# A hybrid delta-net, RWKV and expert layer: two ring sizes, and the place of the first branch's merge products

## The chip, the cores and the metric

The kernel runs on one core of one Trainium2 chip. The metric is the device time of one execution in microseconds (us), and the time of a kernel is the median of its runs. One further execution was profiled; all rows of the trace come from it.

## The reference, cut to what matters

One layer over 256 latent tokens and 256 context tokens of width 1024. A projection feeds two recurrent branches (a gated delta net and RWKV-7), each runs over the context first and then, from the state so reached, over the latent tokens, in both directions. Their outputs are gated and merged, and a mixture of experts follows.

```python
s = s * ge_c[..., None, None] + jnp.einsum('...ck,...cv->...kv', kd_c, v_new)      # delta net, one chunk of 64
v_new = u_c - jnp.einsum('...ck,...kv->...cv', w_c, s)
o_c = jnp.einsum('...ck,...kv->...cv', qd_c, s) + jnp.einsum('...ij,...jv->...iv', qk_c, v_new)
...
y = jax.nn.sigmoid(g_a) * (o_a @ w_o_a) + jax.nn.sigmoid(g_b) * (o_b @ w_o_b)
return y @ w_out
...
hid = jax.nn.silu(jnp.einsum('td,edf->tef', t, w_gate[grp])) * jnp.einsum('td,edf->tef', t, w_up[grp])
out = out + jnp.einsum('tef,efd->td', hid * combine[:, grp, :, None], w_down[grp])
```

There are 32 experts with 3 MB of weights each, and every one is read in full.

## The kernel before

The whole program is unrolled. The code says what is computed in which tiles; a scheduler then fixes each engine's order, by priorities (`hi("gs")` raises one) and by when a pool of tiles finds room in the on-chip memory. Each engine, and the queue SP that issues most of the transfers, works its list strictly in order.

The stages, in the order in which they pass on TensorE (PE):

- Projections of both branches, the RWKV recurrence over the context (`rwkv_step(0, ...)`, four steps) and over the latent tokens (`rwkv_step(1, ...)`, four steps), with the delta net's preparation between them. A latent step multiplies keys with queries (`akps`), masks them on VectorE (DVE) into four tiles of the ring `arb`, forms `rps` and `ups`, copies to `ruv`, and ends with the outputs `yps`. The delta net's key-query products are `kqp`; they read `gq` and `gk`.
- The delta net's eight chunk steps, `gdn_step(0..7)`. A step loads `gkc` and `gvc` (steps 4 to 7 also `gqc`), transposes them on PE (`gkt`, `gvt`), scales them to `gkd` on DVE and `gr` on ScalarE (ACT), subtracts the state's part (`gks`, then DVE on `gr`), solves (`gup`, copied by ACT to `guu`) and updates the state (`gsp`, added on DVE to `gS`, which GpSimd (POOL) has decayed first). Latent steps also make the output `gop`, copied to `gr`, transposed as `got`, added to `yo`. Their tiles live in the pool `gx`, which in the kernel before opens where the recurrence's pools have closed. `gkt`, `gvt` and `got` share a single PSUM buffer.
- Beside these steps, the remaining gate projections (`pj`) and conditioning products (`ada`), whose weights come through a ring of tiles named `w`: 10 tiles of 256 KB in the main pool (`NB['w']`), 12 in a second pool (`w2`) in this stage.
- `rwkv_post`: a norm over the RWKV output (`mean` twice, `ysq`, `yc`) and its gate.
- `merge_b`: the first of the two branches to be merged, eight groups of products `pab` from `yc`, each read by DVE into `tbs`.
- `gdn_post` (`gon`), a small product `shp`, then `merge_a` (`pab` from `post`), the output projection (`acc`), residual and router.
- The experts, four at a time: gather (`xsp`), gate and up (`gup` from `wgu`), down (`dnp` from `wd`). `wgu` has 6 slots of 2 MB and `wd` 7 of 1 MB. Parts of the first experts' weights are loaded ahead, during the merges, where room opens.

`merge_b` is written ahead of the steps, and `gdn_step` has raised priority, so that the scheduler mixes the two.

Of the kernel before, what the change touches and what calls it, by code (L numbers as in the profile page):

```python
# [17 lines left out]
P = 128  # L18
# [82 lines left out]
class K:  # L101
    def __init__(self, ctx, tc, A, dbg=None):
        self.nw = NB["w"]
        self.ctx, self.tc, self.nc, self.A, self.dbg = ctx, tc, tc.nc, A, dbg or {}
# [55 lines left out]
    def e(self, name, *dims, rows=P):  # L160
        return self.t(self.pe, name, *dims, tag="e", bufs=NB["e"], w=520, rows=rows)

    def rt(self, name, *dims):
        return self.t(self.prt, name, *dims, tag="rt", bufs=NB["rt"], w=520)

# [65 lines left out]
    def ada_first(self, hf, pool):  # L231
        ps = self.psum(NB["at"][0], name="ada0")[:, 0:512]

# [8 lines left out]
        self.nc.vector.tensor_copy(a, ps)  # L242
        pt = self.psum(NB["at"][1], name="adat")
        for j in range(4):
# [9 lines left out]
    def ada_rest(self, i, tags):  # L254
# [5 lines left out]
        if q == 0:  # L260
            self.copy(self.arow[b], ps, NB["aa"])
        else:
# [340 lines left out]
    def rwkv_step(self, seg, s, T):  # L603
# [6 lines left out]
        V = X[:, 1024:1536].rearrange("p (j a n) -> p j a n", j=4, a=2)  # L610
# [6 lines left out]
        if upd:  # L617
# [8 lines left out]
            if S is not None:  # L626
                Sp = self.t(self.pst, "rS", 2, 4, C, bufs=1)
                for e in range(2):
                    r = slice(64 * e, 64 * e + 64)
# [5 lines left out]
        nc.vector.tensor_copy(uv[0:64, 1, :], ps[0:64, :])  # L635


        arb = lambda: self.t(self.prx, "arb", 512, bufs=8)
        if seg:
            m = self.cst("mkr").rearrange("p (d x) -> p d x", d=2).unsqueeze(2).to_broadcast([P, 2, 2, 2 * C])  # L640
            rb = [[arb().rearrange("p (d j x) -> p d j x", d=2, j=2) for e in range(2)] for p in range(2)]
            for p in range(2):
                pvs = [self.psum("ch", name="akps").rearrange("p (d j x) -> p d j x", d=2, j=2) for e in range(2)]
                for d in range(2):
                    for j in range(2):
                        for e in range(2):
                            r = slice(64 * e, 64 * e + 64)
# [5 lines left out]
        else:  # L653
            pvs = [self.psum("ch", name="akps")[:, 0:4 * C].rearrange("p (j n) -> p j n", n=C) for e in range(2)]
            for j in range(4):
                for d in range(2):
                    ko = 64 * (1 - d)
                    for e in range(2):
                        r = slice(64 * e, 64 * e + 64)
# [8 lines left out]
        for h in range(8):  # L668
            e, j = h % 2, h // 2
# [20 lines left out]
        if upd:  # L690
# [4 lines left out]
            for h in range(8):  # L695
                r = slice(64 * (h % 2), 64 * (h % 2) + 64)
# [4 lines left out]
            for e in range(2):  # L701
                r = slice(64 * e, 64 * e + 64)
                self.copy(self.RSb[r, :, :, 64 * e:64 * e + 64], sv[r], e)

        if seg:
            yp = self.psum("ch", name="yps")
            yv = yp.rearrange("p (d j n) -> p d j n", d=2, j=4)
            for h in range(8):
                e, j = h % 2, h // 2
                r = slice(64 * e, 64 * e + 64)  # L710
# [269 lines left out]
    def gdn_step(self, s, T, tmp):  # L980
        nc = self.nc
        lat = s >= 4
        S = self.GS
        x = lambda name, *dims, bufs=2, pool=tmp: self.t(pool, name, *dims, bufs=bufs)
        KT, GV, QE = x("gkc", NH, 2, C, bufs=NB["gk"]), x("gvc", NH, 2, C, bufs=NB["gk"]), None
        nc.sync.dma_start(KT, self.kscr[s])
        nc.sync.dma_start(GV, self.vscr[s])
        if lat:
            QE = x("gqc", NH, 2, C, bufs=NB["gq"])
            nc.sync.dma_start(QE, self.escr[s - 4])  # L990
        v4 = lambda x: x.rearrange("p (h n) -> p h n", h=NH)
        ps = self.psum("pp", name="gkt")
        for h in range(NH):
            self.tr(ps[:, h * P:(h + 1) * P], KT[:, h].rearrange("p a n -> p (a n)"))
        kd = x("gkd", NH, P)
        self.tt(kd, v4(ps), self.kdc[:, s, :].unsqueeze(2).to_broadcast([P, NH, P]))
        ps = self.psum("pp", name="gvt")
        for h in range(NH):
            self.tr(ps[:, h * P:(h + 1) * P], GV[:, h].rearrange("p a n -> p (a n)"))
        r1 = x("gr1", NH, P, pool=self.gkeep)  # L1000
        for h in range(NH):
            self.act(r1[:, h, :], ps[:, h * P:(h + 1) * P], scale=self.bt[:, s, h:h + 1])
        if S is not None:
            ps = self.psum("gc", name="gks")
            for h in range(NH):
                for d in range(2):
                    self.mm(ps[64 * d:64 * d + 64, h * P:(h + 1) * P], KT[:, h, d, :], S[:, d, h, :])
            for h in range(NH):
                self.stt(r1[:, h, :], ps[:, h * P:(h + 1) * P], self.nbe[:, s, h:h + 1], r1[:, h, :],
                         ALU.mult, ALU.add)  # L1010
        ps = self.psum("gc", name="gup")
        for h in range(NH):
            for d in range(2):
                r = slice(64 * d, 64 * d + 64)
                self.mm(ps[r, h * P:(h + 1) * P], T[r, s * NH + h, :], r1[r, h, :])
        u = x("guu", NH, P)
        self.act(u, v4(ps))
        if s < 7:
            Sn = x("gS", 2, NH, P)
            if S is not None:  # L1020
                self.tt(Sn, S, self.sdec[:, :, :, s:s + 1].to_broadcast([P, 2, NH, P]), eng=nc.gpsimd)
            pss = [self.psum("gc", name="gsp") for _ in range(2)]

            for h in range(NH):
                for d in range(2):
                    r = slice(64 * d, 64 * d + 64)
                    self.mm(pss[d][:, h * P:(h + 1) * P], kd[r, h, :], u[r, h, :])
            for d in range(2):
                if S is None:
                    nc.vector.tensor_copy(Sn[:, d], v4(pss[d]))  # L1030
                else:
                    self.tt(Sn[:, d], Sn[:, d], v4(pss[d]), ALU.add)
            self.GS = Sn
        if lat:

            ps = self.psum("gc", name="gop")
            for h in range(NH):
                for d in range(2):
                    self.mm(ps[64 * d:64 * d + 64, h * P:(h + 1) * P], QE[:, h, d, :], S[:, d, h, :], start=h == 0,
                            stop=False)  # L1040
            for h in range(NH):
                for d in range(2):
                    r = slice(64 * d, 64 * d + 64)
                    self.mm(ps[r, h * P:(h + 1) * P], self.AQ[r, s - 4, h, :], u[r, h, :], start=False, stop=h == NH - 1)
            o = x("gr1", NH, P, pool=self.gkeep)
            self.act(o, v4(ps))
            ps = self.psum("pp", name="got")
            for h in range(NH):
                self.tr(ps[:, h * P:(h + 1) * P], o[:, h, :])
            pv = ps.rearrange("p (h d n) -> p h d n", h=NH, d=2)  # L1050
            for d in range(2):
                c0 = (s - 4) * C if d == 0 else L - (s - 3) * C
                dst = self.GO[:, :, c0:c0 + C]
                src = pv[:, :, d, :] if d == 0 else pv[:, :, d, ::-1]
                if s < 6:
                    self.act(dst, src)
                else:
                    self.tt(dst, dst, src, ALU.add)
# [388 lines left out]
EP0 = ((("wgu", 1), ("wd", 0)), (("wgu", 2), ("wd", 1)))  # L1447
EP1 = (("wgu", 3), ("wgu", 4), ("wd", 2))
PRE = (("wgu", 0), ("wgu", 1), ("wgu", 2), ("wd", 0), ("wgu", 3), ("wd", 1), ("wd", 2), ("wd", 3))
NB = {'st': 2, 'ys': 'PP', 'yc': [1, 1], 'hn': 'VAVA', 'im': 'AAPP', 'e': 7, 'rt': 13, 'w': 10, 'e1': 4, 'o2': 2, 'kvr': 2, 'cv': 'PVVPPVPPPVVV', 'g1': 3, 'g2': 0, 'imt': 1, 'gi': 0, 'hi': {'p00': 2500, 'p01': 2500, 'i0': 2500, 'gp': 2000, 'R': 2000, 'i': 2000, 'gs': 2000, 'I': 2000, 'J': 2000, 'p11': 200, 'j0': 1500, 'g': 400, 'V': -400, 'rw': 2000}, 'zf': 1, 'g0': 1, 'pe': 0, 'vr': 'vr', 'jt': 'pp', 'go': 'KGGgGGRRGRRikIVGQqJrrrrG', 'rX': 1, 'rbk': 2, 'ixt': 1, 'vh': 2, 'bk': 4, 'ar': 3, 'gm': 7, 'fp': [[28, 'pj'], [29, 'gc'], [20, 'gc'], [21, 'ch'], [22, 'ch']], 'at': ['pp', 'ch'], 'pf': {'ma': 2, 'oo': 0.5}, 'pm': 8, 'aa': 1, 'gr': 0, 'gu': ['pj', 'gc', 'gc'], 'gq': 2, 'gk': 2, 'w2': 12, 'ip': [0, 0, 4], 'gt': ['pj']}  # L1450


def layout(inp):
# [69 lines left out]
def build(tc, A, dbg=None, upto="all"):  # L1523
    def pool(st, name, side="left"):
        return st.enter_context(tc.tile_pool(name=name, bufs=1, side=side, reuse_waits="tile"))

    def hi(n):
        return tc.high_priority(NB["hi"][n]) if n in NB["hi"] else ExitStack()

    with ExitStack() as ctx:  # L1530
        k = K(ctx, tc, A, dbg)
# [6 lines left out]
        with ExitStack() as mix:  # L1538
# [4 lines left out]
            with ExitStack() as ph1:  # L1543
# [6 lines left out]
                with ExitStack() as s:  # L1550
                    lo, kvr = pool(s, "lo"), pool(s, "kvr")
# [31 lines left out]
                gp = pool(chs, "gdn")  # L1583
# [51 lines left out]
                TG, gm = t[2], n["G"]  # L1635
# [6 lines left out]
            gx = k.steps = pool(ctx, "gx", "right")  # L1642
# [11 lines left out]
            with ExitStack() as s:  # L1654
                po = pool(s, "post")
                with hi("po"):
                    y = k.rwkv_post(po)
                with hi("mb"):
                    k.merge_b(y, tbs)
            with hi("gs"):  # L1660
                for i in range(NB["gi"], 8):
                    k.gdn_step(i, TG, gx)
            chs.close()
            k.pw, k.nw = pw, NB["w"]

# [91 lines left out]
```

## Time and profile before

| | us |
|---|---|
| median of 3 runs (882.27 to 888.66) | 888.65 |
| the profiled execution, its own time | 885.67 |
| its span in the trace | 883.9 |
| PE busy | 777.3 |
| DVE busy | 387.4 |
| ACT busy | 229.7 |
| POOL busy | 195.3 |

The profiled execution's time is 1.77 us more than its span. Times below are counted from the span's start. Busy PE includes products that run at either of two granted clocks (1.00 in the tables is 2.4 GHz, 0.50 is 1.2 GHz), so a busy stretch can still be a slow one.

### The profile page before, as it was taken

The numbers are of one execution on the slowest core, as the hardware profiler recorded it, in microseconds if no ns is written. First come the engines' busy times: TensorE is split into PE (matmuls) and PEld (weight loads), VectorE is DVE, ScalarE is ACT, GpSimd is POOL, SyncE is SP. The second block draws the span as 40 slices with busy tenths as digits, with TensorE's granted clock in tenths as the row PEclk, the third lists the DMA queues.
The fourth block names the chain that finished last, engine by engine and source line by source line (L and its number), as shares of the span: only waits on it lengthen the run. The fifth ranks groups of instructions, "written<-read, shape, count | busy, mean of one in ns | idle before, by whom it ended". The sixth has DMA issues, their size and how long they took to land. (4 is left out here: it accounts for less than half of the span.)

```text
span 883.9 us, 14517 instructions
## 1 busy us (share of the span) xinstructions
PE 777.3 (88%) x5833; PEld 457.8 (52%) x5833; DVE 387.4 (44%) x761; ACT 229.7 (26%) x436; POOL 195.3 (22%) x279
## 2 busy tenths in 40 slices
PE   6999899798969999999969998769979997797795
PEld 1444457445447765767856756647445532332231
DVE  1334869996994448944421224333262210111112
ACT  0324626334455224245301213241030000000002
POOL 1013344447344246832201100000120000000000
PEclk8999899798979999999688999987988998999998
DMA  9731455453336652355539994546794999999994
GB/s 347 302 107 61 146 165 178 155 182 135 131 127 205 245 204 75 111 161 160 163 97 378 329 321 125 196 143 214 274 370 162 425 426 425 423 428 423 421 405 181
DMA packets 90085, 210.55 MB, mean 238 GB/s; under 512 B 7944, under 2 KB 37392, under 8 KB 83104
## 3 DMA queue, kind: packets, MB, share of 16 engines
q1 hardware_dynamic: 86976, 205.87, 63.8%
q10 hardware_dynamic: 3040, 3.74, 1.2%
q8 instruction: 46, 0.75, 0.3%
q14 instruction: 23, 0.19, 0.1%
HBM read 189.64 MB, written 19.94 MB: 237 GB/s over the span
## 5 line engine op out<-in xcount | busy, mean ns | idle before, releaser
L107 PE MATMUL pj<-u,w 128*128 128x256 f32 (+1 forms) x768 | 252.2, 483 | 2.6 <-DVE gz L120 2.4
L107 PEld LDWEIGHTS pj<-u,w 128*128 128x128 f32 x768 | 148.0, 198 | 90.5 <-issue 70.2
L107 PE MATMUL gup<-wgu,xs 128*32 128x512 f32 x512 | 75.1, 653 | 16.2 <-DMA wgu<-in_wgu_dram 16.2
L107 PEld LDWEIGHTS gup<-wgu,xs 128*32 128x32 f32 x512 | 19.7, 118 | 68.1 <-issue 42.8
L113 DVE TENSOR_TENSOR msg<-msg,gup 128x256 f32<-128x256 f32 x8 | 3.4, 421 | 113.8 <-ACT msg L123 113.8
L113 POOL TENSOR_TENSOR rl<-rl,mhalf 128x1 f32<-128x1 f32 x2 | 1.1, 547 | 223.6 <-DVE rl L117 223.6
L107 PE MATMUL dnp<-wd,mhT 128*32 128x512 f32 x256 | 43.5, 599 | 4.8 <-DVE mhT L1353 4.1
L113 DVE TENSOR_TENSOR ixt<-ixt,itm 128x31 f32<-128x31 f32 (+22 forms) x89 | 44.8, 504 | 2.0
L113 DVE TENSOR_TENSOR itm<-ixt,imt 128x31 f32<-128x31 f32 (+22 forms) x89 | 39.9, 448 | 2.2
L107 PEld LDWEIGHTS xsp<-oh,h 128*128 128x128 f32 x256 | 33.0, 205 | 7.4 <-issue 7.4
L123 ACT ACT_TABLE_LOAD x24 | 30.8, 1283 | 19.5 <-PE ssq L107 11.0
L107 PE MATMUL xsp<-oh,h 128*128 128x128 f32 x256 | 34.8, 290 | 0.0
L113 POOL TENSOR_TENSOR cacc<-cacc,cm 128x512 f32<-128x512 f32 (+1 forms) x24 | 27.8, 1158 | 27.1 <-ACT cm L123 20.3
L113 POOL TENSOR_TENSOR gS<-gS,sdec 128x1024 f32<-128x1024 f32 x6 | 11.5, 1913 | 96.0 <-PE gop L107 38.8
L107 PE MATMUL acc<-my,ohT 128*128 128x512 f32 x64 | 30.2, 599 | 0.8 <-DVE my L113 0.8
L123 ACT ACTIVATE msg<-gup 128x256 f32<-128x256 f32 x8 | 3.1, 384 | 101.4 <-PE gup L107 101.4
L123 ACT ACTIVATE xs<-xsp 128x512 f32<-128x512 f32 x8 | 4.8, 598 | 94.6 <-PE xsp L107 94.6
L107 PE MATMUL acc<-w,m 128*128 128x512 f32 x64 | 28.3, 592 | 0.0
L113 POOL TENSOR_TENSOR shs<-xp 128x512 f32<-128x512 f32 (+1 forms) x15 | 14.2, 944 | 58.2 <-ACT xp L123 58.2
L117 DVE TENSOR_SCALAR shtm<-pj,omu 128x256 f32<-128x256 f32 x25 | 12.0, 480 | 31.6 <-ACT xp L123 31.6
L113 DVE TENSOR_TENSOR my<-dnp,g 128x512 f32<-128x512 f32 x16 | 11.1, 692 | 31.2 <-PE dnp L107 31.2
L107 PEld LDWEIGHTS dnp<-wd,mhT 128*32 128x32 f32 x256 | 9.8, 109 | 28.2 <-issue 18.9
(373 smaller groups left out, 1267.8 us busy)
## 6 DMA issues: line engine op xcount, KB each, us to landing
wgu<-in_wgu_dram SPq DMA_DIRECT2D x24, 2048.0 KB
wd<-in_wd_dram SPq DMA_DIRECT2D x27, 1024.0 KB
w<-in_w_in_dram SPq DMA_DIRECT2D x96, 256.0 KB
w<-in_ada_w_dram SPq DMA_DIRECT2D x64, 256.0 KB
aw<-in_ada_w_dram SPq DMA_DIRECT2D x16, 512.0 KB
wgu<-in_wgu_dram SPq DMA_DIRECT2D x16, 512.0 KB
rX<-rscr SPq DMA_DIRECT2D x8, 768.0 KB
wgu<-in_wgu_dram SPq DMA_DIRECT2D x20, 256.0 KB
```

What stands on the lines that cost most here:

```text
L107: return self.nc.tensor.matmul(out, lhsT, rhs, start=start, stop=stop)
L113: (eng or self.nc.vector).tensor_tensor(out=out, in0=a, in1=b, op=op)
L117: (eng or self.nc.vector).tensor_scalar(out=out, in0=a, scalar1=s1, scalar2=s2, op0=op0, **kw)
L123: return self.nc.scalar.activation(out=out, in_=in_, func=func, **kw)
```

## The change

Three edits. The ring `arb` of the recurrence has 5 tiles instead of 8. The ring `w` of the main pool has 9 tiles instead of 10. And `merge_b` moves: steps 0 to 6 of the delta net are written ahead of it, its PE products are ordered behind the last product of step 6's state update (`issue_after` adds this order, on PE alone), and step 7 is written behind it.

```diff
-        arb = lambda: self.t(self.prx, "arb", 512, bufs=8)
+        arb = lambda: self.t(self.prx, "arb", 512, bufs=5)
...
-                    self.mm(pss[d][:, h * P:(h + 1) * P], kd[r, h, :], u[r, h, :])
+                    self.lastgdn = self.mm(pss[d][:, h * P:(h + 1) * P], kd[r, h, :], u[r, h, :]).ins
...
-NB = {... 'rt': 13, 'w': 10, 'e1': 4, ...}
+NB = {... 'rt': 13, 'w': 9, 'e1': 4, ...}
...
                 with hi("po"):
                     y = k.rwkv_post(po)
-                with hi("mb"):
+                with hi("gs"):
+                    for i in range(NB["gi"], 7):
+                        k.gdn_step(i, TG, gx)
+
+                with tc.issue_after(k.lastgdn):
                     k.merge_b(y, tbs)
-            with hi("gs"):
-                for i in range(NB["gi"], 8):
-                    k.gdn_step(i, TG, gx)
+                with hi("gs"):
+                    k.gdn_step(7, TG, gx)
```

The pools take less room with the smaller rings, and `gx` no longer waits for the recurrence's pools to close: the step's tiles lie beside them. On PE, up to the first `kqp` product, the order is the same row for row; from there it differs.

PE, at the end of the last latent step, in the kernel before (the numbers behind names tell apart tiles that share a name):

```order
L107 MATMUL yps<-rA,sbd_1497 64x64
L107 MATMUL yps<-arb,ruv 64x64
L110 MATMUL gkt<-cs,gkc 128x128 x4
L110 MATMUL gvt<-cs,gvc 128x128 x4
L107 MATMUL gup<-gr_4468,TG 64x128 x8
L110 MATMUL gkt<-cs,gkc 128x128 x4
L107 MATMUL pj<-u,w 128x256 x8
L107 MATMUL gsp<-guu,gkd 128x128 x8
```

The same place in the changed kernel:

```order
L107 MATMUL pj<-u,w 128x256 x8
L110 MATMUL gvt<-cs,gvc 128x128 x4
L107 MATMUL gup<-gr_4387,TG 64x128 x8
L107 MATMUL ups<-rr_3940,iT 64x64 x15
L110 MATMUL gkt<-cs,gkc 128x128 x4
L107 MATMUL ups<-rr_3940,iT 64x64
L107 MATMUL yps<-rA,sbd_1497 64x64
L107 MATMUL gsp<-guu,gkd 128x128 x8
L107 MATMUL yps<-arb,ruv 64x64
```

Step 0's products, which stood behind the last `yps`, now stand before and among them; step 1's follow among the `yps` too, up to its `gsp` directly ahead of the next `pj`.

SP, a little earlier, at the last `kqp` loads, in the kernel before:

```order
L949 DMA gk<-kscr 128x512
L840 DMA escr<-geg 128x4x128
L949 DMA gq<-qscr 128x512
L949 DMA gk<-kscr 128x512
L949 DMA gq<-qscr 128x512
L272 DMA abr<-in_ada_b_dram 1x512 x4
L275 DMA adascr<-abr 1x512 x4
L346 DMA w<-in_w_out_dram 128x512 x2
L986 DMA gkc<-kscr 128x512
L987 DMA gvc<-vscr 128x512
```

And in the changed kernel:

```order
L949 DMA gk<-kscr 128x512
L986 DMA gkc<-kscr 128x512
L987 DMA gvc<-vscr 128x512
L986 DMA gkc<-kscr 128x512
L987 DMA gvc<-vscr 128x512
L840 DMA escr<-geg 128x4x128
L949 DMA gq<-qscr 128x512
L949 DMA gk<-kscr 128x512
L990 DMA gqc<-escr 128x512
L986 DMA gkc<-kscr 128x512
L990 DMA gqc<-escr 128x512
L949 DMA gq<-qscr 128x512
```

Seven loads of the steps, 256 KB each, have moved ahead of the last `kqp` load.

PE, from the RWKV norm's gate to the merge products, in the kernel before:

```order
L107 MATMUL gate<-bg,g_4334 128x256 x4
L107 MATMUL gop<-gS,gqc 64x128 x8
L107 MATMUL gop<-guu,gdq 64x128 x8
L107 MATMUL gks<-gS,gkc 64x128 x8
L110 MATMUL got<-cs,gr_4752 128x128 x4
L107 MATMUL pab<-yc,w 128x256 x8
L110 MATMUL gkt<-cs,gkc 128x128 x4
L107 MATMUL pab<-yc,w 128x256 x12
L110 MATMUL gvt<-cs,gvc 128x128 x4
L107 MATMUL pab<-yc,w 128x256 x8
L107 MATMUL gup<-gr_4779,TG 64x128 x8
```

The same place in the changed kernel:

```order
L110 MATMUL gvt<-cs,gvc 128x128 x4
L107 MATMUL gup<-gr_4785,TG 64x128 x8
L107 MATMUL gsp<-guu,gkd 128x128 x8
L107 MATMUL pab<-yc,w 128x256 x10
L107 MATMUL gop<-gS,gqc 64x128
L107 MATMUL gks<-gS,gkc 64x128 x8
L107 MATMUL gop<-gS,gqc 64x128 x7
L107 MATMUL gop<-guu,gdq 64x128 x8
L107 MATMUL pab<-yc,w 128x256 x11
L110 MATMUL got<-cs,gr_4845 128x128 x4
L107 MATMUL pab<-yc,w 128x256 x11
L110 MATMUL gkt<-cs,gkc 128x128 x4
```

Before, the `pab` products stood among step 5's; now they stand between step 6's update `gsp` and step 7's first transposes, with step 6's outputs and step 7's `gks` among them. Step 4's outputs, step 5's `gks` and its `gkt` moved too: they now stand ahead of the first `mean`, where before the stretch behind it held step 4's solve, update and outputs.

## Rows read from the trace of the kernel before

**Rows 1.** The page's first line.

```profile
span 883.9 us, 14517 instructions
```

**Rows 2.** Busy us by stretch: PE, PEld, DVE, ACT, POOL; clock, DMA share, GB/s.

```profile
441.87:470.66 28.79, 19.30 (x254) 16.15 (x253) 6.86 (x13) 3.73 (x9) 1.59 (x5) 0.80 0.46 156
470.66:528.41 57.75, 57.64 (x397) 39.37 (x397) 13.29 (x30) 9.96 (x28) 8.12 (x5) 0.98 0.97 346
528.41:600.68 72.27, 55.67 (x433) 42.05 (x430) 27.74 (x59) 24.59 (x41) 3.82 (x2) 0.89 0.53 167
600.68:642.00 41.32, 41.32 (x122) 25.06 (x123) 10.42 (x22) 1.45 (x4) 2.54 (x2) 0.94 0.67 228
642.00:676.00 34.00, 27.37 (x171) 17.77 (x169) 15.37 (x59) 7.70 (x16) 6.08 (x6) 0.85 0.62 247
680.00:840.00 160.00, 135.58 (x829) 55.03 (x824) 24.33 (x58) 5.89 (x12) 0.00 (x0) 0.95 1.01 425
```

**Rows 3.** Timeline of PE: start, duration, products, [idle before, and its releaser].

```profile
444.23 0.69 PE L107 MATMUL kqp<-gq,gk 128*64 128x64 f32 x16 [1.68 <-DMA gq<-qscr]
...
448.15 1.12 PE L107 MATMUL kqp<-gq,gk 128*64 128x64 f32 x16 [2.86 <-DMA gq<-qscr]
...
459.34 0.33 PE L107 MATMUL yps<-arb,ruv 128*64 128x64 f32 x2 [1.07 <-DVE ruv L687]
...
464.83 0.66 PE L110 MATMUL gkt<-cs,gkc 128*128 128x128 f32 x4 [2.45 <-DMA gkc<-kscr]
...
467.84 1.97 PE L107 MATMUL gup<-gr,TG 64*64 64x128 f32 x16 [0.46 <-ACT gr L123]
...
470.66 4.70 PE L107 MATMUL pj<-u,w 128*128 128x256 f32 x16
```

**Rows 4.** The same timeline, later in the projections.

```profile
484.85 1.09 PE L107 MATMUL gup<-gr,TG 64*64 64x128 f32 x16
...
502.63 3.62 PE L107 MATMUL pj<-u,w 128*128 128x256 f32 x16
```

**Rows 5.** Timeline of SP: issues of transfers.

```profile
465.88 1.38 SPq L346 DMA_DIRECT2D w<-in_w_in_dram  x3
...
561.03 2.71 SPq L338 DMA_DIRECT2D wgu<-in_wgu_dram  x6
...
675.61 2.08 SPq L338 DMA_DIRECT2D wgu<-in_wgu_dram  x4
```

**Rows 6.** Shorter stretches, columns as in rows 2.

```profile
560.00:580.00 20.00, 13.96 (x170) 10.62 (x169) 5.62 (x13) 4.42 (x11) 1.91 (x1) 1.00 0.60 208
...
585.00:590.00 5.00, 3.70 (x32) 3.01 (x32) 3.14 (x8) 0.60 (x1) 0.00 (x0) 0.54 0.17 64
...
600.68:605.00 4.32, 4.32 (x10) 3.51 (x11) 0.61 (x3) 0.00 (x0) 0.00 (x0) 0.50 0.14 51
```

**Rows 7.** Timeline, the end of the RWKV norm and the first merge product.

```profile
537.76 3.15 DVE L120 SCALAR_TENSOR_TENSOR yc<-yc,pr,ysq 128x256 f32<-128x256 f32 x4 [2.80 <-ACT ysq L123]
...
543.14 2.10 PE L107 MATMUL pab<-yc,w 128*128 128x256 f32 x7 [3.13 <-DVE yc L113]
```

**Rows 8.** Timeline of PE, steps 6 and 7 and the second merge.

```profile
564.98 1.09 PE L107 MATMUL gks<-gS,gkc 128*64 128x128 f32 x16
...
572.26 1.16 PE L107 MATMUL gsp<-guu,gkd 64*128 64x128 f32 x16 [0.70 <-ACT guu L123]
...
586.30 2.06 PE L107 MATMUL gup<-gr,TG 64*64 64x128 f32 x16 [4.89 <-DVE gr L120]
...
592.87 0.66 PE L110 MATMUL got<-cs,gr 128*128 128x128 f32 x4 [0.70 <-ACT gr L123]
...
600.68 9.73 PE L107 MATMUL pab<-post,w 128*128 128x256 f32 x32
```

**Rows 9.** Waits: on loads of w before 470 us; SP's on PE (total, times, longest).

```profile
  DMA w<-in_w_in_dram: 0.8, 3
...
SPq L346 <- PE pj L107: 135.5, 46, 9.0
```

More of the change, by code (lines that the diff above doesn't have):

```diff
@@ L1449 @@
 PRE = (("wgu", 0), ("wgu", 1), ("wgu", 2), ("wd", 0), ("wgu", 3), ("wd", 1), ("wd", 2), ("wd", 3))
-NB = {'st': 2, 'ys': 'PP', 'yc': [1, 1], 'hn': 'VAVA', 'im': 'AAPP', 'e': 7, 'rt': 13, 'w': 10, 'e1': 4, 'o2': 2, 'kvr': 2, 'cv': 'PVVPPVPPPVVV', 'g1': 3, 'g2': 0, 'imt': 1, 'gi': 0, 'hi': {'p00': 2500, 'p01': 2500, 'i0': 2500, 'gp': 2000, 'R': 2000, 'i': 2000, 'gs': 2000, 'I': 2000, 'J': 2000, 'p11': 200, 'j0': 1500, 'g': 400, 'V': -400, 'rw': 2000}, 'zf': 1, 'g0': 1, 'pe': 0, 'vr': 'vr', 'jt': 'pp', 'go': 'KGGgGGRRGRRikIVGQqJrrrrG', 'rX': 1, 'rbk': 2, 'ixt': 1, 'vh': 2, 'bk': 4, 'ar': 3, 'gm': 7, 'fp': [[28, 'pj'], [29, 'gc'], [20, 'gc'], [21, 'ch'], [22, 'ch']], 'at': ['pp', 'ch'], 'pf': {'ma': 2, 'oo': 0.5}, 'pm': 8, 'aa': 1, 'gr': 0, 'gu': ['pj', 'gc', 'gc'], 'gq': 2, 'gk': 2, 'w2': 12, 'ip': [0, 0, 4], 'gt': ['pj']}
+NB = {'st': 2, 'ys': 'PP', 'yc': [1, 1], 'hn': 'VAVA', 'im': 'AAPP', 'e': 7, 'rt': 13, 'w': 9, 'e1': 4, 'o2': 2, 'kvr': 2, 'cv': 'PVVPPVPPPVVV', 'g1': 3, 'g2': 0, 'imt': 1, 'gi': 0, 'hi': {'p00': 2500, 'p01': 2500, 'i0': 2500, 'gp': 2000, 'R': 2000, 'i': 2000, 'gs': 2000, 'I': 2000, 'J': 2000, 'p11': 200, 'j0': 1500, 'g': 400, 'V': -400, 'rw': 2000}, 'zf': 1, 'g0': 1, 'pe': 0, 'vr': 'vr', 'jt': 'pp', 'go': 'KGGgGGRRGRRikIVGQqJrrrrG', 'rX': 1, 'rbk': 2, 'ixt': 1, 'vh': 2, 'bk': 4, 'ar': 3, 'gm': 7, 'fp': [[28, 'pj'], [29, 'gc'], [20, 'gc'], [21, 'ch'], [22, 'ch']], 'at': ['pp', 'ch'], 'pf': {'ma': 2, 'oo': 0.5}, 'pm': 8, 'aa': 1, 'gr': 0, 'gu': ['pj', 'gc', 'gc'], 'gq': 2, 'gk': 2, 'w2': 12, 'ip': [0, 0, 4], 'gt': ['pj']}
 def layout(inp):
```

## Prediction

> **What bounds the kernel now.** I read first the table of stretches [rows 2]. From 680 to 840 us the transfers run at 425 GB/s with a share of 1.01: the experts are a stream of bytes. Next I read on SP's timeline when that stream starts: at 675.61, when the first four experts' `gup` frees slots [rows 5]. From there to the end of the span [rows 1] are 883.9 - 675.6 = 208.3 us that no PE order changes. So the end moves one for one with the moment at which the first `gup` is done, and that hangs on the chain ahead: last RWKV step, delta-net steps, merges, output projection, router. The reader should see in rows 2 that PE is the busy engine of this chain, but with gaps. From 441.87 (first `kqp`; PE's order is unchanged up to there) to 600.68 (second merge) pass 158.81 us, with PE busy for 19.30 + 57.64 + 55.67 = 132.61 [rows 2]. So 26.2 us are idle: 9.5, 0.1 and 16.6 in the three stretches. The same products are to be worked off there after the change, so all gain comes from these gaps and from the granted clock, which fell to 0.50 to 0.54 at 585 to 605 [rows 6].
>
> **Part 1, the rings.** `arb`: a latent step holds four tiles, and its masks already come behind the former step's last outputs in the unchanged order; zero, bounded by one handoff of 1.07 us either way [rows 3]. `w` from 10 to 9: PE waited for a load of `w_in` 0.8 us in all before 470 us, while SP waited 135.5 us in 46 waits for PE to free a tile [rows 9]. Loads run far ahead of their use; one tile less makes them leave one group of products later. I take zero; what would undo it is a rival below.
>
> **Part 2, steps 0 and 1 beside the last latent step (441.87 to 470.66).** Of 9.49 us idle, 1.68 + 2.86 = 4.54 are waits for `gq` [rows 3]; the other 4.95 (2.45 for the first `gkc`, 1.07 at `yps`, the rest handoffs) lie where step 0 ran alone. Now step 0's and 1's products fill the gaps of `yps`, and these fill theirs: 4.95 go. Of the `gq` waits a `gkt` (0.66 [rows 3]) and some `rps` products fill about 1.0. Against that, the loads of `gq` stand behind up to seven step loads of 256 KB; four of them, ahead of the `escr` write, take 1 MB / 350 GB/s = 2.9 us by the rate of the next stretch [rows 2]. I put 1.2 of these on the path (0 to 2.9), since SP idles there anyway. Clock: after the 2.45 wait `gup` took 1.97 against 1.09 later, and `pj` 4.70 against 3.62 [rows 3, 4]; with one `gkt` and one `gvt` at about 0.45 each over, that is 0.88 + 1.08 + 0.9 = 2.9, gone if PE stays fed. Sum: 4.95 + 1.0 - 1.2 + 2.9 = **7.6** (4 to 9).
>
> **Part 3, the projections (470.66 to 528.41).** Nothing is idle here, and the transfers run at 0.97 [rows 2]: 57.75 us x 346 GB/s = 20 MB. The gate weights cannot start much sooner, since on SP they still stand behind step loads that wait for step 1 and 2 (465.88 before [rows 5], by my count of products about the same after). So I expect this stretch to keep its length and its last `ada` near 527.5. The gain of part 2 shows as work that has left the next stretch: step 4's solve, update and outputs, step 5's `gks` and `gkt` are 1.09 + 1.16 + 2.18 + 1.09 + 0.66 + a `got` of 0.66 = 6.8 us [rows 4, 8]. This is the 7.6 again and is not added.
>
> **Part 4, the merge products behind step 6 (528.41 to 600.68).** Idle before: 16.6. Before, `pab` waited 3.13 us for `yc` [rows 7], and steps 6 and 7 then ran nearly alone, with 4.89 at step 7's `gup` [rows 8]. After: step 5 runs beside the norm. Its state addition on DVE is queued behind three quarters of `yc` (four of 3.15 us together [rows 7]), which waits for ACT; `gks` of step 6 then waits for it: I work out about 4.3 us of idle PE, the old 3.13 at another place and a little more. Step 6 from `gks` to the end of `gsp` took 572.26 + 1.16 - 564.98 = 8.4 us [rows 8], with about 3.1 idle, bare before as after. Then `pab`, about 14 us at full clock (32 products, by the pace of `pj`: 3.62 for eight [rows 4]), covers step 6's outputs and step 7's `gks`. What remains is step 7's tail: some 5 us of idle up to the second merge, since from `got` to the merge 600.68 - 592.87 = 7.8 us pass as before [rows 8]. Idle after: 4.3 + 3.1 + 5.0 = 12.4, so 4.2 go. The clock: step 7's three half-speed groups (`gup` 2.06 [rows 8] against 1.09 [rows 4], and its two output groups by the same factor) go back to full, worth 2.9; I keep 2.0 since the 4.3 wait may cost something at the start of `pab`. Sum: **6.2** (0 to 9). The new order costs nothing where DVE's `tbs` are late: their reader is the second merge, behind step 7.
>
> **Part 5, behind the second merge.** Its first 16 products took 9.73 us at half clock [rows 8, 6] and would take 2 x 3.62 = 7.24 at full: **2.5** (0 to 2.5). I take it, since no wait as long as 4.89 stands near the end any more; the 1.00 granted through 560 to 580, with PE busy for only 13.96 of 20 us [rows 6], says that short waits do not lower it.
>
> **The sum.** 7.6 + 6.2 + 2.5 = 16.3 us. Against the profiled execution's own time that is 885.67 - 16.3 = 869.4; its time stands 3.0 below the median 888.65, so on the median's scale 872. I forecast **871**.
>
> **Rivals.** A: *the clock stays low.* The wait of 4.3 us in step 6 and the bare tail of step 7 hold it at half, as after 4.89 us before [rows 6, 8]. Then part 5 and the clock's 2.0 are lost, and some 3.5 us of `pab` double: the gain is 16.3 - 2.5 - 2.0 - 3.5 = 8.3, on the median's scale 880. For it: the 0.54 behind that wait. Against: 1.00 at 560 to 580. The Trainium skill, in "TensorE: Matmul & The Clock Gate", Part 1, has it that the throttled clock is the default and that activity releases it, which speaks against opening a new gap in step 6; the rows agree for the long wait and do not for the short ones.
>
> B: *the stream eats it.* The early expert loads began at 561.03, when the first merge's tiles came free [rows 5]; after, I expect that at about 569. From 561 to 676 some 39.7 x 167 + 41.3 x 228 + 34 x 247 GB/s = 24 MB were moved [rows 2]. If they go no faster than 247 GB/s they need 99 us, so that `gup` is done at 668 at the earliest: a gain of 8, or, if the first experts' last piece is late, of 4: 880 to 884. Against: there is room up to the 425 of the stream.
>
> C: *it does not do what it says*: the projections are held by the weights' transfers (share 0.97), DVE holds step 5, and gaps only change places: no change, 886 to 889.
>
> D: *slower.* SP is one list, and with 9 tiles a load of `w` that waits for PE holds up what is behind it: the recurrence's own loads. One group of eight `pj` products is 3.62 us [rows 4]; if the loads of seven of the eight recurrence steps leave that much later on the path, 25 us are lost, 9 more than gained: 897. It decides from five steps on (18 us). For it: 46 such waits [rows 9]; against: 0.8 us of PE waits.
>
> **How the numbers follow.** Forecast 0.58, A 0.15, B 0.10, C 0.09, D 0.08. The forecast's own bounds are 4 + 0 + 0 and 9 + 9 + 2.5, so 885 to 868 on the median's scale; a lower edge of 860 allows for gaps that close better than I count. With A and most of B inside, 860 to 885 holds 8 in 10. About 1% (9 us) is what a measurement of this kernel can tell from no change. Faster by over 1% takes the forecast without its poorest sums, and half of A: 0.66; within 1% B, C and the rest of these: 0.25; slower D and a little: 0.09.
>
> **What would show it.** Right: no wait for the first `gkc` behind `yps`; the last `ada` ends at 526 to 529, with step 4's outputs ahead of it; one wait of 3 to 6 us at step 6's `gks` behind DVE; `pab` behind step 6's `gsp` without gaps; second merge at 583 to 589, at a clock of 1.00; the stream's first load behind a freed slot at 657 to 662, and 208 us from there to the end. Wrong: the second merge still near 600, expert loads not landed when the first `gup` starts, or the first `kqp` later than 443, which would put the fault into the smaller weight ring.

## The result, and the profile after

The changed kernel takes 881.17 us (median of 20 runs, 876.44 to 887.34), the kernel before 887.92 us in the runs beside it: a ratio of 0.9944, interval 0.9925 to 0.9963. By this ratio the gain is 5.0 us (3.3 to 6.7), and the forecast said 16.3. (The two medians lie 6.75 us apart; the ratio with its interval is used below.) Its profiled execution took 884.77 us, 3.6 above its own median, while that of the kernel before lay 3.0 below the median of its first three runs. The two traces therefore differ by only 0.9 us, and a comparison of them needs care. The granted clock, as a mean over the whole span, was 0.925 in the 20 runs of the changed kernel, and 0.922 to 0.925 in four sets of runs of the kernel before (77 runs). In those 77, 0.01 of clock went with some 6 us of time.

The stretches of the changed kernel, cut at the same instructions as [rows 2] (first `kqp`, first gate `pj`, first `mean`, second merge; columns as there), with two short ones that answer to [rows 6]:

```profile
span 883.0 us, 14512 instructions
...
440.86:473.43 32.57, 25.67 (x334) 21.41 (x333) 11.44 (x23) 6.38 (x18) 3.51 (x6) 0.90 0.53 172
473.43:531.73 58.30, 58.14 (x405) 38.66 (x405) 10.91 (x24) 8.73 (x23) 8.11 (x5) 1.00 0.93 330
531.73:598.45 66.72, 52.95 (x342) 40.25 (x342) 24.25 (x54) 22.39 (x37) 1.91 (x1) 0.79 0.52 172
...
555.00:560.00 5.00, 4.18 (x33) 3.55 (x34) 0.87 (x5) 1.06 (x3) 0.00 (x0) 0.50 0.17 52
...
598.45:603.00 4.55, 4.55 (x11) 3.66 (x12) 0.70 (x2) 0.00 (x0) 0.00 (x0) 0.50 0.18 66
...
440.86:598.45 157.59, 136.75 (x1078) 100.32 (x1078) 46.59 (x100) 37.51 (x78) 13.53 (x12) 0.89 0.68 230
```

The three stretches hold other shares of the work than before, so they are read as a sum, in the last row: the same 1078 recorded products lie between the first `kqp` and the second merge in both kernels. The kernel before, over the same products (the same view):

```profile
441.87:600.68 158.81, 132.61 (x1078) 97.57 (x1078) 47.89 (x100) 38.28 (x78) 13.53 (x12) 0.91 0.68 230
```

PE's idle time fell from 26.2 to 20.8 us, by 5.4. The same products took 4.1 us longer, at a mean granted clock of 0.89 instead of 0.91, and so the stretch became only 1.2 us shorter. The slowing lies behind the first `mean`: up to there the changed kernel's products took 25.67 + 58.14 = 83.81 us, and before it was 76.94 [rows 2] plus the 6.8 us that moved ahead of the `mean`. The forecast had 8.9 us less of idle time and 4.9 us less of busy time up to this point.

Where the idle time stayed. PE's timeline at the last `kqp` products, which answers to [rows 3]:

```profile
440.86 0.69 PE L107 MATMUL kqp<-gq,gk 128*64 128x64 f32 x16
443.04 0.34 PE L107 MATMUL kqp<-gq,gk 128*64 128x64 f32 x4 [1.50 <-DMA gq<-qscr]
444.45 1.09 PE L110 MATMUL gkt<-cs,gkc 128*128 128x128 f32 x4 [1.07 <-DMA gkc<-kscr]
...
453.35 0.45 PE L107 MATMUL kqp<-gq,gk 128*64 128x64 f32 x8 [2.81 <-DMA gq<-qscr]
...
455.72 4.76 PE L107 MATMUL pj<-u,w 128*128 128x256 f32 x16
...
460.84 1.09 PE L107 MATMUL gup<-gr,TG 64*64 64x128 f32 x16
...
473.43 3.72 PE L107 MATMUL pj<-u,w 128*128 128x256 f32 x16 [0.86 <-DMA w<-in_w_in_dram]
```

The `pj` behind the last `kqp` in the kernel before:

```profile
453.22 3.72 PE L107 MATMUL pj<-u,w 128*128 128x256 f32 x16
```

The wait of 2.45 us for the first `gkc` has shrunk to 1.07, and one of 2.81 us for the last `gq` has come. From the first `kqp` to this `pj` pass 14.9 us; in the kernel before it was 11.4. Most of the difference is work: three of the steps' transposes (`gkt` 1.09, `gvt` 0.66, `gkt` 0.66) now stand here. The waits for `gq` by themselves came to 1.50 + 2.81 = 4.31 us, against 4.54 before. SP's waits and its timeline from 440 to 450 us show what holds the last `gq`:

```profile
SPq L990 <- DMA escr<-geg: 3.7, 1, 3.7
```

```profile
441.86 0.38 SPq L840 DMA_DIRECT2D escr<-geg  x1
442.34 0.45 SPq L949 DMA_DIRECT2D gq<-qscr  x1
443.02 0.32 SPq L949 DMA_DIRECT2D gk<-kscr  x1
447.08 0.32 SPq L990 DMA_DIRECT2D gqc<-escr  x1
447.49 0.38 SPq L986 DMA_DIRECT2D gkc<-kscr  x1
447.93 0.42 SPq L990 DMA_DIRECT2D gqc<-escr  x1
448.40 0.42 SPq L949 DMA_DIRECT2D gq<-qscr  x1
```

The last `gq` load stands behind a `gqc` load that waits until the write of `escr` has landed. That write itself follows four step loads of 256 KB. The wait for the write is not new: in the kernel before, an earlier `gq` load waited for it.

```profile
SPq L949 <- DMA escr<-geg: 2.8, 1, 2.8
```

It has become longer (the waiting load leaves SP 5.2 us after the write, before it was 3.2), and three step loads now pass between it and the last `gq`. So the last `gq` leaves SP 6.5 us after the `escr` write; before it was 4.0 (442.28 and 446.29).

PE's timeline from step 5's update to the second merge, which answers to [rows 7, 8]:

```profile
539.43 1.16 PE L107 MATMUL gsp<-guu,gkd 64*128 64x128 f32 x16
545.04 1.98 PE L107 MATMUL gop<-gS,gqc 128*64 128x128 f32 x16 [4.45 <-DVE gS L113]
...
550.42 0.66 PE L110 MATMUL got<-cs,gr 128*128 128x128 f32 x4
...
555.13 1.97 PE L107 MATMUL gup<-gr,TG 64*64 64x128 f32 x16 [0.84 <-DVE gr L120]
557.80 2.08 PE L107 MATMUL gsp<-guu,gkd 64*128 64x128 f32 x16 [0.70 <-ACT guu L123]
559.80 6.47 PE L107 MATMUL pab<-yc,w 128*128 128x256 f32 x20
...
584.43 1.12 PE L107 MATMUL gup<-gr,TG 64*64 64x128 f32 x8 [1.64 <-DVE gr L120]
...
598.45 10.21 PE L107 MATMUL pab<-post,w 128*128 128x256 f32 x32 [0.89 <-DVE post L113]
```

Step 5's `gop` ran at half clock behind the wait of 4.45 us; step 5's `got` was back at full (0.66); then step 6 ran at half clock again (`gup` 1.97, `gsp` 2.08, against 1.09 and 1.16 at full), and `pab` began so. The second merge's first half took 10.21 us, as slow as the 9.73 before. Not all of it was at half clock (14.5 us would be): the clock was 0.50 in its first 4.55 us, shown above. VectorE's timeline shows the two waits that stand in this tail:

```profile
541.53 1.67 DVE L120 SCALAR_TENSOR_TENSOR yc<-yc,pr,ysq 128x256 f32<-128x256 f32 x4 [5.59 <-ACT ysq L123]
543.12 1.27 DVE L120 SCALAR_TENSOR_TENSOR yc<-yc,pr,bon 128x256 f32<-128x256 f32 x3
544.30 1.28 DVE L113 TENSOR_TENSOR gS<-gS,gsp 128x512 f32<-128x512 f32 x2
...
583.69 0.43 DVE L117 TENSOR_SCALAR rowgate<-rowgate 128x512 f32<-128x512 f32 x1 [1.38 <-DMA rowgate<-adascr]
584.03 0.60 DVE L120 SCALAR_TENSOR_TENSOR gr<-gks,nbe,gr 128x128 f32<-128x128 f32 x2
```

Step 5's state addition stands behind the norm's `yc`. Half of step 7's `gr` stands behind `rowgate`, a row of the later residual that waits for its own load. The forecast knew the first and had overlooked the second, which is in the kernel before too.

### The profile page after: what moved, and what is told of

It is laid out like the page before. It is cut to its first block, busy times and chain, and to the rows that moved or that the text cites. A ratio compares the mean times of both kernels' runs of the same rounds, so it can differ in the third digit from the quotient of the medians.

```text
span 883.0 us, 14512 instructions
## 1 busy us (share of the span) xinstructions
PE 781.5 (89%) x5833; PEld 458.6 (52%) x5833; DVE 386.6 (44%) x761; ACT 228.9 (26%) x436; POOL 193.8 (22%) x279
## 5 line engine op out<-in xcount | busy, mean ns | idle before, releaser
L107 PEld LDWEIGHTS gup<-wgu,xs 128*32 128x32 f32 x512 | 18.5, 121 | 69.8 <-issue 45.7
L113 POOL TENSOR_TENSOR h<-xres,rowscale 128x512 f32<-128x512 f32 x4 | 5.1, 1268 | 93.6 <-DMA w<-in_w_out_dram 81.9
L107 PE MATMUL ada<-aw,silc 128*32 128x512 f32 x64 | 17.8, 717 | 8.3 <-DMA aw<-in_ada_w_dram 8.0
```

What stands on the lines that cost most here:

```text
L107: return self.nc.tensor.matmul(out, lhsT, rhs, start=start, stop=stop)
L113: (eng or self.nc.vector).tensor_tensor(out=out, in0=a, in1=b, op=op)
```

## The experiments

Ratios are to the kernel before in the same job. Busy, idle and clock are from each profiled execution, from the first `kqp` to the second merge; they count one execution and not a median. The job of the result had 887.92 us for the kernel before; the other jobs had 888.89 (runs 1, 2, 3 and 5), 884.51 (4, 6 and 7), 887.25 (8 to 10) and 888.56 (11 and 12), so medians of different jobs are not to be compared, and gains below are taken from the ratios.

| kernel | median | ratio, interval | busy | idle | clock |
|---|---|---|---|---|---|
| before | 887.92 | 1 | 132.6 | 26.2 | 0.91 |
| after | 881.17 | 0.9944, 0.9925 to 0.9963 | 136.8 | 20.8 | 0.89 |
| 1 rings alone | 878.90 | 0.9904, 0.9868 to 0.9940 | 135.2 | 19.8 | 0.89 |
| 2 order alone | 890.28 | 1.0006, 0.9975 to 1.0037 | 140.1 | 25.4 | 0.84 |
| 3 loads behind `gq` | 878.63 | 0.9904, 0.9872 to 0.9936 | 131.9 | 22.1 | 0.90 |
| 4 products in step 5's wait | 879.14 | 0.9930, 0.9900 to 0.9961 | 138.2 | 16.7 | 0.92 |
| 5 state addition first | 879.86 | 0.9893, 0.9842 to 0.9943 | 136.5 | 19.7 | 0.88 |
| 6 = 3 + 5 | 874.66 | 0.9875, 0.9828 to 0.9922 | 132.9 | 18.5 | 0.89 |
| 7 = 1 + the edit of 3 | 876.64 | 0.9898, 0.9863 to 0.9933 | 127.0 | 22.4 | 0.93 |
| 8 `rowgate` later | 877.72 | 0.9874, 0.9846 to 0.9902 | 132.0 | 19.9 | 0.93 |
| 9 = 6 + 8 | 872.70 | 0.9861, 0.9822 to 0.9900 | 132.4 | 15.6 | 0.90 |
| 10 = 9 + products in the tail | 872.44 | 0.9824, 0.9794 to 0.9853 | 131.8 | 17.0 | 0.91 |
| 11 before + the edit of 8 | 886.67 | 0.9976, 0.9943 to 1.0008 | 139.4 | 25.7 | 0.86 |
| 12 = 7 + the edit of 8 | 875.03 | 0.9896, 0.9859 to 0.9933 | 132.0 | 20.1 | 0.89 |

**1 and 2: the change in halves.** Run 1 is the kernel before with both rings smaller; run 2 is the changed kernel with both rings at their old sizes.

```diff
-        arb = lambda: self.t(self.prx, "arb", 512, bufs=8)
+        arb = lambda: self.t(self.prx, "arb", 512, bufs=5)
...
-NB = {... 'w': 10, ...}
+NB = {... 'w': 9, ...}
```

> The two ring sizes alone (5 and 9 tiles), the first branch's merge products where they stood before. Theory 1 (the gain comes from opening the step pool early; the new place of the merge products gives nothing, since its cover is lost to a wait behind VectorE and to a halved clock): as fast as the changed kernel or faster, ratio to the kernel before 0.990 to 0.996, and the second merge's first product at 596 to 599 us. Rival (the moved merge products give the gain, the rings cost as much as they bring): ratio 0.998 to 1.004, and only the order alone is faster.

> The merge products behind step 6's update alone, rings of 8 and 10 tiles as before. Theory 1: no faster than before, ratio 0.998 to 1.006; the wait of 2.45 us for the first step load stays, and steps 5 and 6 run bare behind the norm, with idle TensorE before them and the granted clock at half when the merge products start. Rival: ratio 0.992 to 0.997.

The rings alone give what the whole change gives, or more (the intervals overlap from 0.9925 to 0.9940). The new place of the merge products alone gives nothing that the time shows: 25.4 us of idle time against 26.2. The granted clock has a part in both results: over all their runs it was 0.931 for the rings alone, 0.917 for the order alone, and 0.922 for the kernel before beside them. At some 6 us for 0.01, an estimate from the 77 runs, over half of the 8.5 us of run 1 went with the clock, and the order alone would be some 2 us faster at an equal clock. Why the clock differs between the orders is not shown. Kernels with only one of the rings smaller were not run, so whether both are needed is open. The second merge of run 1 began at 593.27, earlier than the 596 to 599 expected. Run 1 also has the wait of 4.45 us ahead of step 5's `gop`, and 5.85 us ahead of step 7's `gup`, with `pab` in its old place.

**3: the step loads behind the last load of `gq`**, on SP alone.

```diff
+                self.lastgq = self.lastk
...
+        with self.tc.issue_after(self.lastgq):
             nc.sync.dma_start(KT, self.kscr[s])
             nc.sync.dma_start(GV, self.vscr[s])
...
```

> The changed kernel with the loads of the delta-net steps issued only behind the last load of the key-query products. Theory 2 (the seven step loads ahead of it are what kept the gain of the early stretch small: the last key-query group waited 2.81 us, and from the first such product to the next projection passed 14.9 us against 11.4 before): that stretch is back at 11 to 12 us, the wait in it is under 1 us, and the time is 2 to 4 us below the changed kernel's, ratio to the kernel before 0.988 to 0.993. Rival (the wait comes from the write that these loads need, or from what is queued before): the stretch stays at 14 to 15 us and the ratio at 0.994.

The wait at the last `kqp` is gone. PE's timeline there:

```profile
448.54 0.70 PE L107 MATMUL kqp<-gq,gk 128*64 128x64 f32 x8
449.18 0.81 PE L110 MATMUL gkt<-cs,gkc 128*128 128x128 f32 x4
```

From the first `kqp` to the `pj` it takes 12.3 us, and to the `mean` 86.05 us against 90.87 in the changed kernel. The ratio moved from 0.9944 to 0.9904, some 3.5 us, with intervals that just overlap. That the shorter queue ahead of the last `gq` is the cause is not shown: the waits for `gq` that are left are longer (1.76 + 3.17 = 4.93 us against 4.31), what went is 1.07 for `gkc` and 0.86 for the gate weights, and over the whole stretch idle time did not fall (22.1 us against 20.8), while the same products were faster (131.9 against 136.8).

**4: five products, into a PSUM buffer that nobody reads, in step 5's wait.**

```diff
+            if s == 5:
+                with self.tc.issue_after(self.lastgdn):
+                    dps = self.psum("ch", name="dum")
+                    for i in range(5):
+                        self.lastdum = self.mm(dps, self.cst("ones"), self.cs[:, 0:512]).ins
...
+                    with self.tc.issue_after(self.lastdum) if s == 5 else ExitStack():
...
```

> The changed kernel with five products of 512 columns, into a PSUM buffer that nobody reads, put on TensorE between step 5's gsp and gop, where TensorE waited 4.45 us for gS. Theory (that wait takes the clock down, and the thin work of step 6 then doesn't bring it back): with the wait filled, step 5's gop and gks and step 6's gvt, gup and gsp, 10.6 us in the changed kernel (1.97 + 1.97 + 1.64 + 1.01 + 1.97 + 2.08), go back to about 5.5, and the 64 records of pab from 16.4 to about 14.5; some of the 7 us is taken by waits on VectorE, so 874 to 878 against 881.2. Rival (the clock falls in step 6 whether or not there is work ahead of it, or the chain through VectorE and ScalarE sets the pace there): gup 1.97 and gsp 2.08 stay, or their waits grow by what they lose, and the time stays at 880 to 883.

```profile
543.86 4.56 PE L107 MATMUL dum<-cs 128*128 128x512 f32 x10
548.39 1.09 PE L107 MATMUL gop<-gS,gqc 128*64 128x128 f32 x16
...
555.81 1.67 PE L107 MATMUL gup<-gr,TG 64*64 64x128 f32 x16 [0.84 <-DVE gr L120]
558.18 2.08 PE L107 MATMUL gsp<-guu,gkd 64*128 64x128 f32 x16 [0.69 <-ACT guu L123]
```

Half of the theory holds: behind the filled wait `gop` and `gks` ran at full clock (1.09, against 1.98 and 1.64). But the clock fell one step later, behind waits of 0.75, 0.78 and 0.84 us. A long wait is not needed for it, and the rival's `gsp` of 2.08 is there too. The time is the changed kernel's within the intervals (0.9930 and 0.9944).

**5: step 5's state addition ahead of the norm's scalings on VectorE.** The steps are written ahead of the norm, and the four scalings wait for the addition.

```diff
+            with self.tc.issue_after(self.lastS):
+                self.stt(yc[:, j, :], yc[:, j, :], self.par("lg", j), sq[:, j, :], ALU.mult, ALU.mult)
```

> The changed kernel with one change of VectorE's order: step 5's two state additions stand ahead of the norm's four scalings instead of behind seven of its eight operations. Theory 3 (TensorE's wait of 4.45 us behind step 5's update comes from that queue, and the halved clock of step 6 and of the first merge products from the wait): the wait falls under 2 us, the granted clock is 0.9 or more from step 6 to the merge products, and the time is 4 to 8 us below the changed kernel's, ratio 0.985 to 0.990. Rival (the clock falls anyway, since the small products of steps 5 and 6 do not hold it, or the wait only moves to step 6's scaled keys, queued behind the norm): clock at 0.5 to 0.7 there and less than 2 us gained, ratio 0.992 to 0.996.

The wait ahead of `gop` fell to 0.84 us; 2.13 us appeared at step 6's `gvt`, whose `gkd` now stood behind the norm. So the place of the wait was read rightly, and half of it is saved. The clock went as the rival had it: step 6's `gup` took 1.97 and `gsp` 2.08, and `pab` began at half clock. The gain of 4.5 us by the ratios (0.9944 and 0.9893, intervals overlapping) is what the theory said, but its second half, the clock from step 6 to the merge products, failed.

**6 and 7: the repairs together, and the first of them in the old order.**

> The changed kernel with both repairs: the delta net's step loads issued behind the last load of gq, and step 5's state addition ahead of the RWKV norm's scalings on VectorE. Theory (two separate losses): no wait for gq at the last kqp group (first kqp to mean 86 us, not 91), and less than 1.5 us of wait ahead of step 5's gop, so mean to the second merge at 64 to 66 us; 876 to 878, a ratio of about 0.987. Rival (both repairs only move the same idle time towards step 7's end, which is tied to other engines): 878 to 880, as each alone.

> The kernel before with both smaller rings, its old place of the first merge, and the step loads issued behind the last load of gq. Theory (all that is won comes from the early opening of the step pool, and the new place of the merge products adds nothing): the rings alone gave 878.9; without the wait for gq at the last kqp group (first kqp to mean 86 us, not 90) this comes to 875 to 877, at or below the changed kernel with the same repair (878.6). Rival (the new place is worth something once the loads stand right): it stays at 878 to 881, above 878.6.

Run 6 has the ratio of the theory, 0.9875, and 18.5 us of idle time, and the wait ahead of step 5's `gop` is 0.84 us. Its two parts missed in opposite ways: 89.45 us instead of 86 from the first `kqp` to the `mean` (a wait of 0.82 us for the last `gq` stayed, and the granted clock there was 0.92 against 0.96 in run 3), and 61.9 instead of 64 to 66 from there to the second merge, with step 6 at full clock (`gup` 1.22, `gsp` 1.16). Run 7 equals run 3: with the same repair, the old and the new place of the merge products cannot be told apart (0.9898 and 0.9904).

**8: `rowgate` behind step 7's `gr`.**

```diff
                 if n == "gate1":
-                    self.ts(x, x, 0.5, ALU.mult)
+                    with self.tc.issue_after(self.lastgr):
+                        self.ts(x, x, 0.5, ALU.mult)
```

> The changed kernel with VectorE's scaling of rowgate, which waits for its load, ordered behind step 7's last subtraction gr; in the changed kernel it stands between the two halves of gr, and TensorE's gup of step 7 waited 0.84 and 1.64 us. Theory (the wait of 4.89 us in the kernel before and what is left of it here come from this load, not from the steps running bare): step 7's gup follows its first half without a wait beyond 0.9, and the second merge starts 1.6 to 3 us earlier after step 7's first product; 878 to 880 against 881.2. Rival (step 7's chain through VectorE, ScalarE and the norm sets the pace, so that the wait only moves to the outputs): gup closes up, but the second merge stays where it is, 880 to 882.

```profile
578.79 1.21 PE L107 MATMUL gup<-gr,TG 64*64 64x128 f32 x16 [0.84 <-DVE gr L1009]
579.93 1.09 PE L107 MATMUL gop<-gS,gqc 128*64 128x128 f32 x16
```

Step 7's `gup` closed up. From step 7's `gvt` to the second merge it takes 15.59 us (577.29 to 592.88) instead of 17.85 (580.60 to 598.45): 2.3 us, as expected. The measured gain, 0.9944 to 0.9874, is larger. The rest may lie in the clock, which is not shown: in this execution the same wait of 4.46 us ahead of step 5's `gop` was followed by step 6's `gup` at 1.21 and `gsp` at 1.16, and over its six runs the mean granted clock of the span was 0.929, before it was 0.925.

**9 and 10: all three repairs, and two unread products in the gap ahead of the last `gon`.**

> Both repairs (loads behind gq, step 5's state addition ahead of the scalings) and the scaling of rowgate behind step 7's gr. Theory (three separate waits of other work on a queue ahead of the steps): 2 to 3 us below the two repairs, which had 0.9875 of before: a ratio of 0.983 to 0.986, first gup of the experts 216 to 218 us after the first kqp. Rival (the tail hangs on ScalarE and the norm): 0.986 to 0.989, as the two repairs.

> The three repairs, and two products of 512 columns into a PSUM buffer that nobody reads between step 7's got and the last gon, where TensorE waits 1.5 us. Theory (the gap there holds the granted clock at half through the small products of the bias and the first half of the second merge): with the gap filled, the first 32 records of the second merge take 7.3 to 8 us instead of 9.7, and the run is 1 to 2 us below the three repairs. Rival (the clock falls on what lies before or behind, as in the run with products in step 5's wait, where it fell one step later): 9 to 10 us for the second merge's first 32 records, and the same time as the three repairs or up to 1 us more.

Run 9 has 15.6 us of idle time, 10.6 less than before, and its gain is 12 us (1 - 0.9861 of 887.25). Its ratio stands between the theory's range and the rival's, and its interval reaches over run 6's 0.9875, so what `rowgate` adds to the two repairs is not resolved. The experts' first `gup` came at 653.99 and the span ended at 868.7, 214.7 us later; in the changed kernel it was 216.0. In run 10 the rival holds for the clock: the wait of 2.45 us for `gon` shrank to 0.16, but 1.23 and 1.31 us appeared behind it, and the second merge's first 32 records still took 9.41 us. Its ratio of 0.9824 is lower than run 9's 0.9861, with intervals that overlap.

```profile
584.48 1.88 PE L107 MATMUL dum<-cs 128*128 128x512 f32 x4
586.52 1.12 PE L107 MATMUL gon<-yo,cs 128*128 128x512 f32 x2 [0.16 <-ACT yo L123]
...
589.03 2.37 PE L107 MATMUL shp<-wr,shc 128*128 128x36 f32 x16 [1.23 <-DVE shc L1170]
592.71 1.65 PE L107 MATMUL pab<-post,w 128*128 128x256 f32 x3 [1.31 <-DVE post L113]
```

**11 and 12: the `rowgate` edit in the old order, without and with the small rings and the loads behind `gq`.**

> The kernel before with one edit, VectorE's scaling of rowgate ordered behind step 7's last subtraction gr. Theory (the wait of 4.89 us at step 7's gup came from rowgate's load, not from step 7 running bare, so that a part of what the forecast took from the new place of the merge products belongs to this load): that wait falls to 0.8 to 0.9, the second merge starts 3 to 4 us earlier after step 7's gvt, 884 to 885 against 888.6, a ratio near 0.996. Rival (bareness: step 7's chain hangs on the norm's load or on ScalarE): the wait goes to gop or got, and the ratio is 0.999 to 1.001.

> The kernel before with both rings smaller, the old place of the merge products, the step loads behind gq, and the scaling of rowgate behind step 7's gr. Theory (the new place of the merge products is worth nothing that can be measured once these two waits are away): 0.984 to 0.988 of before, as the three repairs in the new order (0.986, interval 0.982 to 0.990). Rival (the new place hides step 6's outputs and is worth 2 us or more): 0.989 or above.

The theory of run 11 was wrong in part. Of the 4.89 us [rows 8], 3.37 stayed. ScalarE's timeline of run 11 shows what stands there, step 7's `gr` behind the norm of the middle rows with its two table loads:

```profile
588.55 1.28 ACT L123 ACT_TABLE_LOAD   x1
589.84 0.69 ACT L123 ACTIVATE yo<-gon,eps 128x512 f32<-128x512 f32 x1
590.55 1.28 ACT L123 ACT_TABLE_LOAD   x1
591.84 0.63 ACT L123 ACTIVATE yo<-yo 128x512 f32<-128x512 f32 x1
592.38 1.12 ACT L123 ACTIVATE gr<-gvt,gcolb 128x128 f32<-128x128 f32 x4
```

In the new order `gr` passes ahead of the second table load (run 8: 0.84 us at `gup`); in run 12, in the old order, PE still waited 1.08 + 2.11 us there. So the new place does clear ScalarE for step 7, and `rowgate` hid that. Run 12's ratio of 0.9896 is in the rival's range and not in the theory's, but its interval holds both, so what the new place is worth was not resolved: run 9, which also has the edit of 5, has 0.9861.

Run 11 also gives the size of the chance in one trace. Its PE order in this stretch is that of the kernel before, yet the same products took 6.8 us longer:

```profile
443.03:608.08 165.05, 139.40 (x1078) 102.87 (x1078) 47.41 (x99) 38.24 (x78) 13.15 (x11) 0.86 0.65 222
```

Its profiled execution took 892.47 us, 6.8 more than the 885.67 of the kernel before, just this difference.

## Why the prediction was wrong

The direction was right, and the sum of 16.3 was three times too large. The forecast of 871 is also 1 us below what the sum gives (872). By its steps:

- **What bounds the kernel.** Held. From the slot that frees the stream's first load (674.11) to the end pass 208.9 us, as the 208.3 before, and in run 9 the end moved with the first `gup`. Rival B, the stream eating the gain, is refuted by run 9: its first `gup` came 14.5 us earlier than before (653.99 against 668.5), had its weights without a wait, and from there to the end passed 214.7 us (215.4 before).
- **Part 1, the rings at zero cost.** Held: run 1 lost nothing. Rival D is refuted by it.
- **Part 2, 7.6 us.** Idle time in this stretch fell from 9.5 to 6.9 where the forecast had 4.7. The waits for `gq` came to 4.3 us, forecast 4.54 - 1.0 + 1.2 = 4.7, so this term held in size, though its working knew only the loads' bytes and not the wait for the `escr` write. Mis-sized were the other 4.95, taken as gone: 2.6 were there after the change, 1.07 at the first `gkc`, 0.66 for ScalarE's `guu` of step 1 and 0.86 at the first gate weights. The 2.9 for the clock came where it was looked for (step 0's `gup` took 1.09, the first gate `pj` 3.72) and was lost beside it: the `pj` behind the wait of 2.81 us took 4.76 instead of 3.72, and step 0's `gkt` 1.09 instead of 0.66. The sum of the products up to the `mean` shows none of it (83.8 us both before and after).
- **Part 3, unchanged length, last `ada` near 527.5.** 58.30 us against 57.75, so held, but shifted: the last `ada` ended at 531.8. The work that was to leave the next stretch, 6.8 us from step 4's solve to step 5's `gkt`, did move ahead of the `mean`. The gate weights did not start at about the same time: they left SP at 469.08, 3.2 us later than before, behind a step load of `gkc` that had waited 6.6 us for step 1's `gks`.
- **Part 4, 6.2 us.** The wait for step 5's state addition was foreseen in size (4.45, forecast 4.3); it ended ahead of `gop` and not of `gks`, since `gsp` holds both buffers `gc` until the addition. Idle time came to 13.8, forecast 12.4; the wait of 1.64 us behind `rowgate`, not foreseen, is of that size. The 2.0 for the clock turned into a loss: step 6 and the start of `pab` ran at half clock, the place that rival A named. Behind the `mean` the same products took some 4.1 us longer (52.95 against 55.67 - 6.8).
- **Part 5, 2.5 us.** Wrong: the second merge began at 0.50 in the changed kernel, and its first half took 9.1 to 9.8 us in runs 6 to 10 too. The premise, that no long wait near the end means full clock, fails in runs 4, 9 and 10, where nothing above 1.9 us stood directly ahead of half-clock work in step 6 or, in run 10, the second merge.

The failed step is the granted clock, 7.4 us of the 16.3 (2.9 + 2.0 + 2.5), taken from [rows 3, 6, 8] of one execution as half-clock work that a better fed PE would get back. On balance none of it came: single groups returned to full clock and others fell to half. The runs say the same as the trace. By the 77 runs before, 7.4 us would be some 0.012 of mean clock (an estimate); the changed kernel's 0.925 lies 0 to 0.003 above those sets. What came is idle time, 5.4 of the 8.9, and the measured gain of 5.0 is of this size. The missing 3.5 of idle time are, from part 2, the 2.6 us of other waits, less 0.4 by which `gq` was better than forecast, and from part 4 the wait behind `rowgate`. That the slower products of the changed kernel's trace (136.75 against 132.61) are due to the change is not shown, since run 11 differs more without it.

Rival A's 880 lies near the measured median, and half clock in step 6, in `pab` and in the second merge is what it foresaw. That its time came so near is in part luck: it kept part 2's 2.9 for the clock and all of the 8.9 us of idle time.

The Trainium skill, in "TensorE: Matmul & The Clock Gate", Part 1, says that the throttled clock is the default and activity lifts it. The trace agrees for the long wait: behind the 4.45 us `gop` ran at half clock, and after `gop` and `gks` the clock was back at full in `got`. For short waits the traces go both ways: among waits of 0.70 to 1.19 us the clock was 1.00 in the kernel before [rows 6], and among waits of 0.70 and 0.84 us it was 0.50 in the changed kernel from 555 to 560 us. The forecast had taken the first as the rule.

What stays open: what takes the clock to half at the start of the second merge in all fourteen traces (its first 32 records took 8.6 to 10.2 us, against 7.24 at full clock), and why step 6 ran at full clock in two executions of the new order (runs 6 and 8) and not in the others.

## What to carry to other kernels

Count the gain of a new order in idle time of the bounding engine over a stretch that holds the same work in both kernels, and give the clock's share no more than a place in the range: it changed by more between two executions of one order (0.91 and 0.86, the kernel before and run 11) than by the edit. Idle time of one trace is no full account either: run 3 has more of it than the changed kernel (22.1 us against 20.8) and a lower ratio. Read it beside the busy time, and beside the mean clock of many runs. Before counting a wait as the bare pace of a chain, read every instruction ahead of the late one on its engine's queue, and ahead of the late load on the DMA queue; a wait there for quite another thing (`escr`, `rowgate`) can stay when the work around it is moved. An edit that opens a pool earlier also moves that pool's loads ahead in the queue, and their own dependences come with them.

## What was not expected of the hardware

The same 1078 products took between 127.0 us (run 7, mean granted clock 0.93) and 140.1 us (run 2, 0.84) in profiled executions. Filling a wait of 4.45 us with work moved the fall of the clock by one step and did not prevent it (run 4). The mean granted clock of many runs moves with the order of the products, too: 0.931 with the rings alone (0.927 to 0.936 in 10 runs), 0.917 with the order alone (0.911 to 0.929 in 12 runs). ScalarE's table loads, 1.28 us each, stood twice on the path of step 7 in the old order (run 11).
